# A DiT block pair on one core: attention in one written order with two-bank PSUM tiles, modulation units beside the block pairs, and the last norm in two halves

## The chip, the core and the metric

The kernel runs on one core of one Trainium2 chip. The metric is the device time of one execution in microseconds (us). The kernel before took 1587.46 us, the median of three runs (1584.85 to 1589.65). A profile is one more execution, recorded by the hardware profiler; its span runs from the first to the last instruction, and the execution's own time lies a little above it.

## What is computed

Two layers on 256 latent tokens and 256 context tokens of width 1024. Layer 0 is swiglu, short convolution, swiglu; layer 1 is swiglu, grouped-query attention (8 query heads of 128, 2 key/value heads, 512 keys), swiglu. Layer 1 after the attention works on the latent tokens alone. Cut to what matters here:

```python
mod  = (silu(c) @ mod_w[i] + mod_b[i])          # shift, scale, gate for each of three sublayers
modc = (silu(c_ctx) @ mod_w[i] + mod_b[i])      # the same for the context stream
...
lat = lat + 0.5 * gate * swiglu(rms(lat) * g * (1 + scale) + shift, w13, w2)
...
q = rope(rms(h @ w_q)); k = [rms(hc @ w_k), rope(rms(h @ w_k))]; v = [hc @ w_v, h @ w_v]
p = softmax(q k^T / sqrt(128))
lat = lat + gate * ((p v) @ w_o)
...
lat = lat + 0.5 * gate * swiglu(rms(lat) * g * (1 + scale) + shift, w13, w2)
```

Everything is float32. A product is made on TensorE from operands that are each split in a high part (rounded to fp32r by a copy on ScalarE) and a low part (the rest, a subtraction on VectorE); three matmuls (high*high, high*low, low*high) add up to one product.

## The kernel before

Activations are kept transposed, as eight tiles of 128 features by tokens. Each weight tile of 1 MB comes by DMA from the SP queue (load_raw, L92, three buffers), is split (split, L97) by ScalarE at L98 and VectorE at L99 into halves "wh" and "wl" of 1024 columns (four buffers of each), and is used by mm3 (L118), three matmuls at L122 to L124. An engine runs its instructions in one order, which a scheduler made ahead of time out of the program's text by its own estimate of times; an instruction that waits holds all behind it on its engine. Where the text says tc.manual_schedule, the named engines keep the order of the text.

**Modulation.** The 224 modulation units are VectorE dot products of 128x1024 (mod_unit, L136, instruction at L142, tile "junk"), whose weights go through the same raw buffers. next_unit (L169) issues one; tick(n) (L179) adds n to what is owed and issues units while one is owed; mod_ready (L186) issues whatever a value still lacks. Ticks stand in the projections (1.5 or 1.9 an output tile), in the convolution (6 a tile), four in the attention's projections, 2 a head in the attention, 1 an output tile in the attention's output projection, and 1 a block in the last swiglu.

**Block pairs.** In the three swiglus on 512 tokens most of the hidden blocks are worked with seven products of half size instead of eight (class Pair, L539): head, five, six, seven and four each issue products and the small VectorE and ScalarE steps between them. In the loop of ffn (L611) the pair before is finished (seven, four) amid the products of the next.

**Attention.** PSUM is divided into six one-bank tiles (psm) and two (pss). For each head, scores (L1033) makes two 128x512 score tiles "psc" (one per query tile), for each the row maximum (L1042), the scaled negative of it (L1044), the exponential with its row sum on ScalarE (L1050), a reciprocal (L1054) and the division on POOL (L1058). turn (L1062) transposes the probabilities by eight matmuls into "pt" and splits them (L98, L99); mix (L1078) multiplies with the values into "pav" and splits the result into "a". Projections of the values (v_proj, L966) for the context tokens stand between the first heads. The text runs two heads of scores ahead; the scheduler picked the order. Then wo, the output projection: eight output tiles "py" of 24 matmuls each, each added to x (gated, L1119), after which x, scaled but not yet normed, is split into "xa".

**The last swiglu.** 22 blocks. The first four (first_mm, L1170) work on "xa", so that they can begin before the norm is known, and are corrected afterwards by the reciprocal of the norm "rl" (first_post, L1194). In block 1 the norm is made (rms_inv), and after it the normed operand "h": for each of eight tiles a product on VectorE (L256), a shift on ScalarE (L1226) and a low part on VectorE (L1227). From block 4 on, mm2 (L1106) does with "h" and one 512-column matmul (L1107) and one of 256 (L1108) what takes three elsewhere.

Of the kernel before, what the change touches and what calls it, by code (L numbers as in the profile page):

```python
# [9 lines left out]
F32 = mybir.dt.float32  # L10
# [6 lines left out]
P = 128  # L17
D = 1024
KT = D // P
S = 256  # L20
# [7 lines left out]
EPS = 1e-6  # L28
WARM = 36
# [12 lines left out]
def hybrid_kernel(ctx: ExitStack, tc: tile.TileContext, a: dict, out: bass.AP):  # L42
# [7 lines left out]
    psm = ctx.enter_context(tc.tile_pool(name="psm", bufs=6, space=bass.MemoryType.PSUM))  # L50
    pss = ctx.enter_context(tc.tile_pool(name="pss", bufs=2, space=bass.MemoryType.PSUM))
# [8 lines left out]
    def psum(s="ps"):  # L60
        return psm.tile([P, T2], F32, tag="mm", name=nm(s))

    def psmall(s="pq"):
        return pss.tile([P, T2], F32, tag="sm", name=nm(s))
# [114 lines left out]
    def tick(n):  # L179

        owed[0] += n
        while (jobs or units) and owed[0] >= 1:
            owed[0] -= 1
            next_unit()
# [348 lines left out]
    class Pair:  # L533
# [66 lines left out]
        def seven(self):  # L600
            self.prod(self.p, "S3", "T3", False)
            nc.vector.tensor_tensor(
                out=self.u[:, S:], in0=self.p, in1=self.gm[:, S:], op=ALU.add
            )
# [300 lines left out]
    pqs = pss.tile([P, T2], F32, tag="sm", name="pqs")  # L905
# [60 lines left out]
    def v_proj(tt):  # L966
        if tt % 2 == 0:
            vt.append(new_pair("v"))
        ps = psum("pv")
# [62 lines left out]

    def scores(hd):  # L1033
        kv = hd // (HEADS // KVH)
        r_ = []
        for qt in range(2):
            o = (hd % 2) * S + qt * P
            ps = psum("psc")
            mm3(ps, tuple(t[:, o : o + P] for t in qs[hd // 2]), ks[kv], True, True)
            ci = hd * 2 + qt  # L1040
            mx = ap.tile([P, 1], F32, name=nm("mx"), tag="mx", bufs=4)
            nc.vector.reduce_max(mx, ps, axis=AX.X)  # L1042
            nb = ap.tile([P, 1], F32, name=nm("nb"), tag="nb", bufs=4)
            nc.vector.tensor_scalar(  # L1044
                out=nb, in0=mx, scalar1=scq[:, ci : ci + 1], scalar2=-1.0,
                op0=ALU.mult, op1=ALU.mult,
            )
            e = tp.tile([P, T2], F32, name=nm("e"), tag="sg", bufs=3)
            sm = ap.tile([P, 1], F32, name=nm("sm"), tag="smx", bufs=4)
            nc.scalar.activation(  # L1050
                out=e, in_=ps, func=AF.Exp, scale=scq[:, ci : ci + 1], bias=nb, accum_out=sm
            )
            r = ap.tile([P, 1], F32, name=nm("r"), tag="r", bufs=4)
            nc.vector.reciprocal(r, sm)  # L1054
            if qt == 0:
                pn2 = hot("pn", F32)
            pn = pn2[:, qt * T2 : qt * T2 + T2]
            nc.gpsimd.tensor_scalar(out=pn, in0=e, scalar1=r, scalar2=None, op0=ALU.mult)  # L1058
            r_.append(pn)
        return r_  # L1060

    def turn(pn):  # L1062
        pth, ptl = (hot(t).rearrange("p (b q) -> p b q", q=S) for t in ("pth", "ptl"))
        for qt in range(2):
            pt = psum("pt")
            for kt in range(4):
                nc.tensor.transpose(
                    pt[:, kt * P : kt * P + P], pn[qt][:, kt * P : kt * P + P], ident
                )
            split(  # L1070
                pth[:, :, qt * P : qt * P + P], ptl[:, :, qt * P : qt * P + P],
                pt.rearrange("p (k q) -> p k q", k=4),
            )
        return pth, ptl

    aos, at = [], []

    def mix(hd, pt):  # L1078
# [4 lines left out]
        po = psum("pav")  # L1083
        for kt in range(4):
            vw = tuple(t[:, kv * P : kv * P + P] for t in vs[kt])
            mm3(po[:, :S], vw, (pt[0][:, kt, :], pt[1][:, kt, :]), kt == 0, kt == 3)
        o = (hd % 2) * S
        ah, al = (t[:, o : o + S] for t in at[-1])
        split(ah, al, po[:, :S])
        aos.append((ah, al))  # L1090

    pns, pts = {0: scores(0)}, {}
    v_proj(2)
    v_proj(3)
    pns[1] = scores(1)
    for hd in range(HEADS):
        if hd + 2 < HEADS:
            pns[hd + 2] = scores(hd + 2)
        pts[hd] = turn(pns.pop(hd))
        if hd:  # L1100
            mix(hd - 1, pts.pop(hd - 1))
        tick(2)
    mix(HEADS - 1, pts.pop(HEADS - 1))


# [32 lines left out]
    wo = by_pairs("wo")  # L1138
    for m in range(KT):
        if m == KT - 2:  # L1140
            ready()
        w = wo(m)
        ps = psum("py")
        for k in range(KT):
            mm3(ps[:, :S], w(k), aos[k], k == 0, k == KT - 1)
        gated(m, ps[:, :S], gate)
        square_add(m, 0, S)
# [10 lines left out]
        tick(1)  # L1158
# [46 lines left out]
    ht = []  # L1205
    for i in range(NM):
# [3 lines left out]
        if i < 4:  # L1210
# [6 lines left out]
            if i == 1:  # L1217
                for q in range(4):
                    t = hot("h")
                    ht.append(t)  # L1220
                    for k in (2 * q, 2 * q + 1):
                        o = (k % 2) * T2
                        hi, lo = t[:, o : o + S], t[:, o + S : o + T2]
                        u = scaled(0, k, A, ris)
                        b = B[:, k, :1]
                        nc.scalar.activation(out=hi, in_=u, func=AF.Identity, bias=b)  # L1226
                        nc.vector.scalar_tensor_tensor(  # L1227
                            out=lo, in0=u, scalar=b, in1=hi.bitcast(F32),
                            op0=ALU.add, op1=ALU.subtract,
                        )  # L1230
# [120 lines left out]
```

## Time and profile before

| | |
|---|---|
| runs | 1584.85, 1587.46, 1589.65 us |
| the profiled execution's own time | 1589.78 us |
| its span | 1588.0 us |
| mean granted TensorE clock | 0.995 |
| VectorE busy | 1319.8 us (83%) |
| ScalarE busy | 738.2 us (46%) |
| POOL busy | 29.8 us (2%) |

A line of the timeline reads: start, duration, engine, operation and source line, the tile written and those read, shapes, and how many instructions were merged; in square brackets stands how long the engine had been idle before, and what ended that. Times of a merged line run from the first start to the last end. Matmul durations include a pipeline's latency, so that consecutive matmuls overlap; how far apart they start is what counts.

### The profile page before, as it was taken

To read this page: it belongs to the slowest core of one execution; us is meant where nothing else is said; L and a number is where in the kernel's file an instruction comes from. 1 tells how busy PE (TensorE), PEld (TensorE's weight loads), DVE (VectorE), ACT (ScalarE), POOL (GpSimd) and SP (SyncE) were. 2 spreads that over 40 slices of the span, in tenths; PEclk is the share of its full clock that TensorE was granted. 3 is DMA by queue.
4 is the path that set the end of the run, shared out by engine and by line. 5 is a ranking of instruction groups with operands and counts; after the bars stand their busy time and mean duration, and the time that the engine had idled before them with its cause. 6 is when DMAs were issued, how large, how long until landed. Compare 5 with 4: busy or idle time off the path is not lost.

```text
span 1588.0 us, 25040 instructions
## 1 busy us (share of the span) xinstructions
PE 1565.0 (99%) x10210; PEld 1423.9 (90%) x10210; DVE 1319.8 (83%) x2029; ACT 738.2 (46%) x1180; POOL 29.8 (2%) x20
## 2 busy tenths in 40 slices
PE   8999999999999999999999999999999999899998
PEld 6788998998888899989899899899899898888887
DVE  5778778879998879799798899898898899976654
ACT  5532452544322356335345375335255455655543
POOL 0000000000000000000000000000000005200000
PEclk9999999999999999999999999999999999999999
DMA  8545234234565412452342423443433654645552
GB/s 319 181 174 201 92 115 167 104 117 162 186 214 193 177 65 95 142 200 104 130 177 102 160 103 107 158 161 107 175 133 122 235 186 149 234 156 186 186 202 90
DMA packets 38419, 248.74 MB, mean 157 GB/s; under 512 B 5280, under 2 KB 7072, under 8 KB 11936
## 3 DMA queue, kind: packets, MB, share of 16 engines
q1 hardware_dynamic: 35712, 245.38, 43.5%
q10 hardware_dynamic: 2592, 1.76, 0.4%
q8 instruction: 80, 1.31, 0.3%
q14 instruction: 35, 0.29, 0.1%
HBM read 244.77 MB, written 1.05 MB: 155 GB/s over the span
## 4 chain that ended last, share of the span: by engine, by line
PE 93%; DVE 3%; ACT 2%; DMA 1%; issue 1%; POOL 0%; DVEq 0%; POOLq 0%; ACTq 0%
PE py L122 9%; PE py L123 9%; PE py L124 9%; PE p L124 7%; PE p L123 7%; PE p L122 7%; PE q L122 5%; PE q L123 5%; PE q L124 5%; PE py L1107 3%; PE pg L1107 2%; PE pu L1107 2%; PE pg L122 2%; PE pg L123 1%; PE pg L124 1%; PE pu L124 1%
## 5 line engine op out<-in xcount | busy, mean ns | idle before, releaser
L98 ACT ACTIVATE wh<-wr 128x1024 fp32r<-128x1024 f32 (+2 forms) x276 | 277.2, 1015 | 352.2 <-PE py L123 81.2
L99 DVE TENSOR_TENSOR wl<-wr,wh 128x1024 fp32r<-128x1024 f32 (+2 forms) x276 | 319.7, 1166 | 78.4 <-ACT wh L98 71.0
L142 DVE CUSTOM_DVE_ANT_0 junk<-wr,scbc,modb 128x1024 bf16<-128x1024 f32 x224 | 286.8, 1280 | 25.0 <-DMA wr<-in_modT 22.2
L123 PE MATMUL py<-gl,wh 128*128 128x512 f32 (+1 forms) x570 | 213.3, 374 | 0.0
L122 PE MATMUL py<-gh,wh 128*128 128x512 f32 (+1 forms) x570 | 213.3, 374 | 0.0
L124 PE MATMUL py<-gh,wl 128*128 128x512 f32 (+1 forms) x570 | 213.0, 374 | 0.0
L99 DVE TENSOR_TENSOR wl<-ws,wh 128x1024 fp32r<-128x1024 f32 x108 | 131.3, 1223 | 28.6 <-ACT wh L98 28.1
L98 ACT ACTIVATE wh<-ws 128x1024 fp32r<-128x1024 f32 x108 | 113.4, 1058 | 75.1 <-DVE ws L563 32.5
L124 PEld LDWEIGHTS py<-gh,wl 128*128 128x128 f32 x570 | 107.3, 188 | 19.1
L122 PEld LDWEIGHTS py<-gh,wh 128*128 128x128 f32 x570 | 107.4, 188 | 18.5
L123 PEld LDWEIGHTS py<-gl,wh 128*128 128x128 f32 x570 | 107.4, 188 | 18.2
L123 PE MATMUL p<-tl,wh 128*128 128x256 f32 x432 | 122.2, 283 | 0.0
L124 PE MATMUL p<-th,wl 128*128 128x256 f32 x432 | 122.2, 283 | 0.0
L122 PE MATMUL p<-th,wh 128*128 128x256 f32 x432 | 122.2, 283 | 0.0
L122 PE MATMUL q<-bh,wh 128*128 128x256 f32 x320 | 90.6, 283 | 0.0
L123 PE MATMUL q<-bl,wh 128*128 128x256 f32 x320 | 90.6, 283 | 0.0
L124 PE MATMUL q<-bh,wl 128*128 128x256 f32 x320 | 90.6, 283 | 0.0
L122 PEld LDWEIGHTS p<-th,wh 128*128 128x128 f32 x432 | 82.9, 192 | 0.3
L123 PEld LDWEIGHTS p<-tl,wh 128*128 128x128 f32 x432 | 82.9, 192 | 0.3
L124 PEld LDWEIGHTS p<-th,wl 128*128 128x128 f32 x432 | 82.9, 192 | 0.0
L446 DVE SCALAR_TENSOR_TENSOR x<-py,G,x 128x256 f32<-128x256 f32 x144 | 62.9, 477 | 6.3 <-PE py L124 6.0
L557 DVE TENSOR_TENSOR ws<-wr 128x1024 f32<-128x1024 f32 x54 | 65.7, 1218 | 0.0
(296 smaller groups left out, 4181.1 us busy)
## 6 DMA issues: line engine op xcount, KB each, us to landing
wr<-in_w SPq DMA_DIRECT2D x88, 1024.0 KB, 4.9
wr<-in_modT SPq DMA_DIRECT2D x64, 1024.0 KB, 4.8
wr<-in_w2b SPq DMA_DIRECT2D x24, 896.0 KB, 4.6
wr<-in_w2a SPq DMA_DIRECT2D x12, 1024.0 KB, 4.8
wr<-in_mod SPq DMA_DIRECT2D x8, 1024.0 KB, 6.1
wr<-in_cw_cx SPq DMA_DIRECT2D x8, 1024.0 KB, 4.8
wr<-in_w2l SPq DMA_DIRECT2D x8, 1024.0 KB, 4.8
wr<-in_cw_b SPq DMA_DIRECT2D x4, 1024.0 KB, 4.9
```

Source lines behind the costliest of these rows:

```text
L98: nc.scalar.activation(out=hi, in_=src, func=AF.Copy)
L99: nc.vector.tensor_tensor(out=lo, in0=src, in1=hi.bitcast(F32), op=ALU.subtract)
L122: nc.tensor.matmul(ps, wh, mh, start=first, stop=False, **kw)
L123: nc.tensor.matmul(ps, wh, ml, start=False, stop=False, **kw)
L124: nc.tensor.matmul(ps, wl, mh, start=False, stop=last, **kw)
L142: nc.vector.tensor_tensor_reduce(out=junk, in0=raw[:, j * D : j * D + D], in1=scbc[:, v, :], scale=1.0, scalar=modb[:, l, col : col + 1], ...
L446: nc.vector.scalar_tensor_tensor(out=x[:, m, s * S : s * S + S], in0=ps[:, o : o + S], scalar=g[:, m, s : s + 1], in1=x[:, m, s * S : s * ...
L557: tt(out=sm.rearrange("p (a b c) -> p a b c", a=2, b=2)[:, :, 0, :], in0=a21.unsqueeze(1).to_broadcast([P, 2, T2]), in1=self.raw[:, T2 : 3 ...
L1107: nc.tensor.matmul(ps, w[0], m, start=first, stop=False, skip_group_check=True)
```

## The change

- A pool of PSUM can be closed and another opened in its place (use_banks); the option reuse_waits="tile" makes a new tile wait for the old tiles that it overlaps. During the attention PSUM is two score tiles of two banks each, one transposition tile of two banks, and two one-bank tiles for the products with the values. After the second output tile of wo the old division comes back.
- scores makes both query tiles into one two-bank tile, with one row maximum of 128x2x512, one negation and one reciprocal for both. The division on POOL is in place. turn, rest, out_hi and out_lo are the parts of the two splits.
- TensorE, VectorE and ScalarE follow the text's order through the whole attention, the first two tiles of wo included. wo's first weights are loaded and split ahead of it; a one-column exponential ahead of it loads the table.
- The ticks of the attention and of wo go; a tick of 0.5 comes behind the addition in seven in the block pairs' loop, queued right behind that addition.
- In the last swiglu five blocks work on "xa" instead of four. The normed operand is made in two halves, after blocks 1 and 2 and behind their corrections: for a half, one product on VectorE of 128x1024, for each tile two shifts on ScalarE (one rounded, one not), and for each two tiles one subtraction on VectorE.

```diff
+FIRST = 5
+ORDERED = {mybir.EngineType.PE, mybir.EngineType.DVE, mybir.EngineType.Activation}
...
+    def use_banks(*pools):
+        stage.close()
+        for name, bufs in pools:
+            banks[name] = stage.enter_context(
+                tc.tile_pool(
+                    name=name, bufs=bufs, space=bass.MemoryType.PSUM, reuse_waits="tile"
+                )
+            )
+
+    use_banks(("psm", 6), ("pss", 2))
...
-    def tick(n):
+    def tick(n, behind=None):
...
+            if behind is None:
+                next_unit()
+            else:
+                with tc.issue_after(behind.ins):
+                    next_unit()
...
-                        prev.seven()
+                        tick(0.5, prev.seven())
...
+    warm = ap.tile([P, 1], F32, name="warm", tag="warm", bufs=1)
+    nc.scalar.activation(out=warm, in_=scq[:, :1], func=AF.Exp, scale=0.0)
+    use_banks(("psc", 2), ("ptp", 1), ("pav", 2))
...
+    wo = by_pairs("wo")
+    w01 = [wo(m) for m in range(2)]
...
     def scores(hd):
...
+        ps = double("psc", "psc")
         for qt in range(2):
...
+            mm3(ps[:, qt, :], tuple(t[:, o : o + P] for t in qs[hd // 2]), ks[kv], True, True)
+        nc.vector.reduce_max(mx, ps, axis=AX.X)
...
+    with tc.manual_schedule(engines=ORDERED):
+        scores(0)
+        scores(1)
+        exps(0)
+        exps(1)
+        v_proj(2)
+        scores(2)
+        turn(0, 0)
+        rest(0, 0)
+        exps(2)
+        v_proj(3)
+        turn(0, 1)
+        rest(0, 1)
+        for hd in range(1, HEADS):
+            turn(hd, 0)
+            if hd + 2 < HEADS:
+                scores(hd + 2)
+            turn(hd, 1)
+            rest(hd, 0)
+            if hd > 1:
+                out_hi(hd - 2)
+                out_lo(hd - 2)
+            rest(hd, 1)
+            if hd + 2 < HEADS:
+                exps(hd + 2)
+            mix(hd - 1)
+        py2 = double("psc", "py")
...
+        out_hi(HEADS - 2)
+        out_lo(HEADS - 2)
+        wo_mm(0, range(6))
+        mix(HEADS - 1)
+        out_hi(HEADS - 1)
+        out_lo(HEADS - 1)
+        wo_mm(1, range(6))
+        for m in range(2):
+            wo_mm(m, range(6, KT))
...
-        tick(2)
...
         gated(m, ps[:, :S], gate)
+        if m == 1:
+            use_banks(("psm", 6), ("pss", 2))
...
-        tick(1)
...
+    def norm_half(hf):
+        u = hot("u", F32)
+        ks = slice(4 * hf, 4 * hf + 4)
+        nc.vector.tensor_tensor(
+            out=u.rearrange("p (k t) -> p k t", k=4), in0=x[:, ks, :S],
+            in1=ris.unsqueeze(1).to_broadcast([P, 4, S]), op=ALU.mult,
+        )
+        for q in range(2):
...
+            for j in range(2):
...
+                nc.scalar.activation(
+                    out=t[:, j * T2 : j * T2 + S], in_=u[:, c], func=AF.Identity, **kw
+                )
+                nc.scalar.activation(out=u[:, c], in_=u[:, c], func=AF.Identity, **kw)
...
-        if i < 4:
+        if i < FIRST:
...
             if i:
                 for one in held:
                     first_post(*one, ris)
                 held = []
+            if i in (1, 2):
+                norm_half(i - 1)
```

In the new functions turn(hd, qt) issues the four transpositions of one query tile and the ScalarE copy that is its high part, rest(hd, qt) the VectorE subtraction that is its low part, exps(hd) two exponentials, one reciprocal and the two divisions on POOL, out_hi and out_lo the two parts of the split of a head's result.

More of the change, by code (lines that the diff above doesn't have):

```diff
@@ L968, in v_proj @@
             vt.append(new_pair("v"))
-        ps = psum("pv")
+        ps = psum("pv") if tt < 2 else banks["pav"].tile([P, T2], F32, tag="t", name=nm("pv"))
         for k in range(KT):
@@ L1036, in scores @@
         for qt in range(2):
             o = (hd % 2) * S + qt * P
[L1038 to L1046, printed above, removed]
-            )
@@ L1058, in scores @@
[L1058 to L1072, printed above, removed]
-            )
-        return pth, ptl
@@ new lines, in exps @@
+    def exps(hd):
+        ps, nb = es[hd]
+        sc = scq[:, 2 * hd : 2 * hd + 2]
+        e = es[hd] = hot("e", F32)
+        sm = ap.tile([P, 2], F32, name=nm("sm"), tag="smx", bufs=3)
+        for qt in range(2):
+            nc.scalar.activation(
+                out=e[:, qt * T2 : qt * T2 + T2], in_=ps[:, qt, :], func=AF.Exp,
+                scale=sc[:, qt : qt + 1], bias=nb[:, qt : qt + 1],
+                accum_out=sm[:, qt : qt + 1],
+            )
+        r = ap.tile([P, 2], F32, name=nm("r"), tag="r", bufs=3)
+        nc.vector.reciprocal(r, sm)
+        for qt in range(2):
+            c = slice(qt * T2, qt * T2 + T2)
+            nc.gpsimd.tensor_scalar(
+                out=e[:, c], in0=e[:, c], scalar1=r[:, qt : qt + 1], scalar2=None, op0=ALU.mult
+            )
@@ new lines, in turn, with rest @@
+    def turn(hd, qt):
+        e = es[hd]
+        if qt == 0:
+            pts[hd] = hot("pth"), hot("ptl"), double("ptp", "pt")
+        hi, pt = pts[hd][0], pts[hd][2]
+        for kt in range(4):
+            nc.tensor.transpose(
+                pt[:, qt, kt * P : kt * P + P],
+                e[:, qt * T2 + kt * P : qt * T2 + kt * P + P], ident,
+            )
+        nc.scalar.activation(
+            out=hi[:, qt * T2 : qt * T2 + T2], in_=pt[:, qt, :], func=AF.Copy
+        )
+    def rest(hd, qt):
+        hi, lo, pt = pts[hd]
+        c = slice(qt * T2, qt * T2 + T2)
+        nc.vector.tensor_tensor(
+            out=lo[:, c], in0=pt[:, qt, :], in1=hi[:, c].bitcast(F32), op=ALU.subtract
+        )
@@ L1082, in mix @@
             at.append((t[:, :T2], t[:, T2:]))
-        po = psum("pav")
+        po = pos[hd] = banks["pav"].tile([P, T2], F32, tag="t", name=nm("po"))
+        by_k = [t.rearrange("p (q k t) -> p k q t", q=2, k=4) for t in pts[hd][:2]]
+        p3 = po[:, :S].rearrange("p (q t) -> p q t", q=2)
         for kt in range(4):
             vw = tuple(t[:, kv * P : kv * P + P] for t in vs[kt])
-            mm3(po[:, :S], vw, (pt[0][:, kt, :], pt[1][:, kt, :]), kt == 0, kt == 3)
+            mm3(p3, vw, tuple(t[:, kt] for t in by_k), kt == 0, kt == 3)
@@ L1087, in mix @@
         o = (hd % 2) * S
[L1088 to L1101, printed above, removed]
-        tick(2)
-    mix(HEADS - 1, pts.pop(HEADS - 1))
+        aos.append(tuple(t[:, o : o + S] for t in at[-1]))
@@ L1141, in hybrid_kernel @@
             ready()
[L1142 to L1145, printed above, removed]
+        if m < 2:
+            ps = py2[:, m, :]
+        else:
+            w = wo(m)
+            ps = psum("py")
+            for k in range(KT):
+                mm3(ps[:, :S], w(k), aos[k], k == 0, k == KT - 1)
         gated(m, ps[:, :S], gate)
+        if m == 1:
+            use_banks(("psm", 6), ("pss", 2))
         square_add(m, 0, S)
```

75 lines of the change are left out of this document (41 added, 34 removed).

## The prediction

> **What bounds the kernel now.** The first thing read was the page's busy times.
>
> ```profile
> span 1588.0 us, 25040 instructions
> PE 1565.0 (99%) x10210; PEld 1423.9 (90%) x10210; DVE 1319.8 (83%) x2029; ACT 738.2 (46%) x1180; POOL 29.8 (2%) x20
> ```
>
> TensorE (PE) is busy in 1565.0 of 1588.0 us. The change removes no product, so it can win only where PE stands idle (at most 23 us, some of it at start and end) or runs at a lower clock. Second came the list of PE's waits; three of its rows:
>
> ```profile
> PE pg L1107 <- ACT wh L98: 3.2, 1, 3.2
> PE pt L1067 <- POOL pn L1058: 3.0, 3, 2.0
> ...
> PE py L124 <- DVE wl L99: 1.4, 1, 1.4
> ```
>
> The largest lie in the two stages that the change rewrites: the attention (transpositions waiting for POOL, wo waiting for its weights' low half) and the last swiglu. The third view was the timeline of PE in the attention.
>
> ```profile
> 1319.72 0.40 PE L123 MATMUL psc<-kl,qh 128*128 128x512 f32 x1
> ...
> 1334.74 0.83 PE L1067 MATMUL pt<-ident,pn 128*128 128x128 f32 x4 [1.96 <-POOL pn L1058]
> ...
> 1336.87 0.41 PE L124 MATMUL pav<-pth,vl 128*128 128x256 f32 x1
> 1337.08 0.41 PE L122 MATMUL pav<-pth,vh 128*128 128x256 f32 x1
> ...
> 1345.04 0.63 PE L1067 MATMUL pt<-ident,pn 128*128 128x128 f32 x4 [1.04 <-DVE ptl L99]
> 1345.55 0.39 PE L122 MATMUL pav<-pth,vh 128*128 128x256 f32 x1
> 1345.78 0.28 PE L123 MATMUL pav<-ptl,vh 128*128 128x256 f32 x1
> ...
> 1346.97 0.28 PE L124 MATMUL pav<-pth,vl 128*128 128x256 f32 x1
> 1347.09 0.40 PE L122 MATMUL psc<-kh,qh 128*128 128x512 f32 x1
> ...
> 1348.25 0.40 PE L124 MATMUL psc<-kh,ql 128*128 128x512 f32 x1
> ...
> 1367.53 0.39 PE L124 MATMUL py<-a,wl 128*128 128x256 f32 x1 [1.43 <-DVE wl L99]
> ```
>
> What the reader is to see: 256-column matmuls start 0.119 us apart (1345.78 to 1346.97, ten steps), 512-column ones 0.232 (1347.09 to 1348.25, five steps), four transpositions take 0.51. After the idle 1.96 us the matmuls start 0.21 apart: the clock has fallen too. After idle stretches of 1.04 and 1.43 it has not. The other engines' rows for the same stage:
>
> ```profile
> 1344.22 1.28 DVE L99 TENSOR_TENSOR ptl<-pt,pth 128x512 fp32r<-128x512 f32 x2
> 1344.82 0.68 DVE L99 TENSOR_TENSOR ptl<-pt,pth 128x512 fp32r<-128x512 f32 x1
> 1345.41 0.41 DVE L99 TENSOR_TENSOR a<-pav,a 128x256 fp32r<-128x256 f32 x1
> ...
> 1350.12 1.28 DVE L1042 TENSOR_REDUCE mx<-psc 128x1 f32<-128x512 f32 x2
> 1351.32 0.33 DVE L1044 TENSOR_SCALAR nb<-mx,scq 128x1 f32<-128x1 f32 x2
> 1351.57 1.27 DVE L142 CUSTOM_DVE_ANT_0 junk<-wr,scbc,modb 128x1024 bf16<-128x1024 f32 x1
> ...
> 1329.75 0.77 ACT L1050 ACTIVATE e<-psc,nb,scq 128x512 f32<-128x512 f32 x1
> 1332.87 1.07 ACT L98 ACTIVATE pth<-pt 128x512 fp32r<-128x512 f32 x2
> L1058 POOL TENSOR_SCALAR pn<-e,r x16: 1561/1566/2642, 1325.9 to 1360.3; 128x512 f32<-128x512 f32 x16
> ```
>
> VectorE (DVE) spends 1.2 us on a modulation unit between steps that PE waits for; the text puts sixteen there.
>
> **The attention, rewritten.** A head costs PE 8 transpositions (1.02), 6 score matmuls (1.39) and 12 of 0.119 (1.43), together 3.8 us; POOL 2 x 1.57 = 3.1; ScalarE two exponentials (1.6), two copies (1.07) and one smaller copy, about 3.0. DVE has, in the order written, the maximum of 1024 columns (two of 512 take 1.20 to the next start; I take 1.16), one negation (0.12, half of 1351.32 to 1351.57), a subtraction (0.60, the step 1344.22 to 1344.82), the smaller one for the head two back (0.34, an estimate from its 0.41 less the 0.07 by which such steps overlap) and a last subtraction (0.68). None of these sums is the period, because a loop runs through two engines: the transposition tile has one buffer, so the next head's first transposition waits for the last subtraction of this head, and that stands on DVE behind the maximum, which waits for the scores, which PE issues behind the first transpositions. Around it: 0.14 from the subtraction's end to PE (1344.22 + 0.68 = 1344.90 to 1345.04), 0.51, scores to their end 1.56 (1347.09 to 1348.25 + 0.40), 1.16, 0.12, 0.60, 0.34, 0.68: **5.1 us a head**, with PE idle for 1.3 of them. It holds for the five heads 1 to 5. For head 6 there are no scores: 0.14 + 1.02 + 0.54 (copy, half of 1.07) + 0.34 + 0.34 + 0.68 = 3.1, I take 3.2.
>
> Before the loop: at 1319.72 four matmuls of the first scores are left (0.93), then the second scores (1.39), a value projection of 24 matmuls (2.86), scores (1.39), transpositions (0.51), projection (2.86), transpositions (0.51), copy, subtraction and the way back (0.54 + 0.68 + 0.14): 1331.5. Five periods and 3.2: 1360.2. From there PE runs through to the second wo tile: 0.14 + 1.02 + 12 + 18 + 12 + 18 + 12 matmuls (72 x 0.119 = 8.57) = 9.7: 1369.9. The third wo tile takes PSUM that the first two held, so it waits for the second's addition to x, a DVE step of the 128x256 kind: 0.41 + 0.14 and the last matmul's tail (0.28 - 0.12), 0.7 us of new wait: 1370.6. In the trace of before, the last swiglu's first matmul gives the same point (its row stands below): 1390.5 less six tiles of 24 matmuls (17.1) = 1373.4. **The attention gains 2.8 us**, and its expected larger gain is eaten by the loop of 5.1.
>
> Unknown is on which old tile the first score tile's banks fall; if on the last value projection's, its eviction comes first, 0.54 + 0.68 + 0.14 = 1.4 at most, and nothing if not. I take nothing, since the old tiles are eight and one is late. wo's earlier weights cost nothing that I can place: ScalarE and DVE do those splits anyway. The exponential's table is loaded once in both.
>
> **Modulation.** By a count through the text, 24 ticks go and 46 half ticks (6 + 6, 5 + 6 + 6, 5 + 6 + 6 calls) come, 23 units; by the end of the attention's projections 216 units are issued where 206 were. The 216 are all that wo needs; the last eight fall into mm2 blocks. What they meet there and in the pairs:
>
> ```profile
> L142 DVE CUSTOM_DVE_ANT_0 junk<-wr,scbc,modb 128x1024 bf16<-128x1024 f32 x224 | 286.8, 1280 | 25.0 <-DMA wr<-in_modT 22.2
> ...
> 720.00:760.00 40.00, 40.00 (x336) 40.00 (x335) 36.67 (x47) 23.25 (x37) 0.00 (x0) 1.00 0.29 100
> 720.00:760.00 40.00, 0.00 (x0) 1.00 0.29 100
> ...
> 1445.00:1500.00 55.00, 55.00 (x314) 47.70 (x313) 36.32 (x59) 32.50 (x59) 0.00 (x0) 1.00 0.54 182
> ```
>
> The second and third rows are one stretch of pairs, all engines and then the units alone: PE 40.00, DVE 36.67, no unit. A pair is 84 matmuls, 10.0 us; half a unit each is 4 x 0.5 x 1.2 = 2.4 more, 39.1 of 40. That still fits, and part of the 36.67 is work ahead for the projection, so I take 0; the bound is a whole unit each, 28 us, and gets a rival. In the mm2 stretch DVE is busy 36.32 of 55, so eight units and their four loads of 1 MB (transfer engines half busy, 0.54) lie beside PE.
>
> **The last swiglu.** The rows of PE, DVE and ScalarE there:
>
> ```profile
> L122 PE MATMUL pg<-xa,wh x32: 276/282/419, 1390.5 to 1419.5; 128*128 128x258 f32 x32
> ...
> 1412.90 0.50 PE L1107 MATMUL pg<-h,wh 128*128 128x512 f32 x1 [3.18 <-ACT wh L98]
> 1413.59 0.40 PE L122 MATMUL pu<-xa,wh 128*128 128x258 f32 x1
> ...
> 1417.01 0.30 PE L124 MATMUL pg<-xa,wl 128*128 128x258 f32 x1
> ...
> 1420.47 0.40 PE L1107 MATMUL pg<-h,wh 128*128 128x512 f32 x1
> 1420.82 0.40 PE L1107 MATMUL pu<-h,wh 128*128 128x512 f32 x1
> ...
> 1401.73 1.28 DVE L256 SCALAR_TENSOR_TENSOR t<-x,A,rl 128x256 f32<-128x256 f32 x3 [1.21 <-ACT rl L1214]
> 1411.88 1.22 DVE L99 TENSOR_TENSOR wl<-wr,wh 128x1024 fp32r<-128x1024 f32 x1
> ...
> 1405.52 1.30 ACT L1226 ACTIVATE h<-t,mod 128x256 fp32r<-128x256 f32 x3
> 1406.84 1.28 ACT L1200 ACT_TABLE_LOAD   x1
> 1411.81 1.04 ACT L98 ACTIVATE wh<-wr 128x1024 fp32r<-128x1024 f32 x1
> ```
>
> PE stands 3.18 us in block 3, whose low weights ("wl") start on DVE only at 1411.88, behind ten microseconds of norm and corrections; then sixteen matmuls take 1413.59 to 1417.01, 3.42 where 1.90 is usual: 1.5 more. Together 4.7. After the change DVE has before block 3's weights two corrections (four steps of some 0.35 each, 2.8) and one half of the norm (1.16 + 2 x 0.60 = 2.4): from 1401.73 to 1406.9; the weights end at 1409.2. PE wants them after three blocks of 48 matmuls and 0.45 for the norm's own, 1390.5 + 17.6 = 1408.1. So about **1.1 us of wait stay**, too little for the clock to fall. ScalarE sets the other bound: table 1.28, eight shifts 3.4, two corrections 1.4, two weight halves 2.0 from 1401.7 end at 1409.8, DVE's last half at 1411.0: 2.9 of wait and perhaps the clock again. The fifth early block costs 48 x 0.119 = 5.71 against sixteen steps of 0.35 (1420.47 to 1420.82) = 5.60: 0.1. The gain is 4.7 - 1.1 - 0.1 = **3.5**, between 0.2 and 4.6.
>
> **The sum**: 1588.0 - 2.8 - 3.5 = 1581.7 for the span; 1.78 lie around the span in the profiled execution (1589.78), which was 2.3 above the median, so against the median 1587.46 - 6.3 = **1581.2 us**.
>
> **Rivals.** *Shorter loop.* If the transposition tile comes free bank by bank, its first bank waits only for the first subtraction: 0.34 + 0.68 drop out, 4.1 a head, five times 1.0: 1576.2. For it: every instruction that touches the tile keeps to one bank. Against: a tile is one thing to its pool.
>
> *The wait at the end stays.* The norm now takes twice the ScalarE shifts (16 instead of 8, 3.4 us more), on the engine that the 3.18 us row names: 3.3 of the 3.5 lost, 1584.5.
>
> *The clock.* PE is idle 1.3 us in every period. Only the 1.96 us gap was followed by a low clock here, 1.43 was not; but these repeat. At 0.21 instead of 0.119 a step the 0.51 and 1.39 on the loop grow by some 1.5, five times: 1588.7. The Trainium skill, TensorE: Matmul & The Clock Gate, bears on both sides: its Part 1 says that a wholly idle window of about 3.4 us lowers the clock, which the 1.96 us gap here contradicts; its paragraph on a second failure mode says that short idle spells between groups of matmuls can make the clock swing.
>
> *Slower: units beside the pairs hold PE.* A unit queued right behind the addition delays by 1.2 us the weight splits behind it; PE, at 40.00 of 40, has no slack to make it good. If half of each of 23 units shows, 13.8 us: 1595.0. It decides from 0.48 us a unit (11 us, the gain and the bound below). For: DVE at 36.67 without any. Against: the weights have four buffers, and runs of units now pass the projections without a PE wait.
>
> **Chances.** What a measurement of this kernel can tell from no change is about 0.3%, 4.8 us: below 1582.7 is faster. The forecast 0.40 (1578 to 1585: 0.28 faster, 0.12 same), shorter loop 0.25 (faster), wait stays 0.10 (same), clock 0.10 (same), units 0.15 (slower). Faster 0.53, same 0.32, slower 0.15. The range reaches from the short loop with all of the last wait gone (1576.2 - 1.1, and 2 for the other waits of the attention) to the clock with a third of the last rival's price: 1573 to 1593.
>
> **What would show it.** Right: PE's wait for the transposition tile names the second subtraction, transpositions of one head start 5.1 apart, the wo tile after the second waits some 0.7, the 3.18 us row is near 1.1 and no slow matmuls follow it. Pairs show no PE wait and no DVE share of 40 in 40. Wrong: periods of 4.1, matmuls 0.21 apart inside the attention, or PE waits on "wl" in the pairs.

## The result, and the profile after

The changed kernel takes 1599.7 us, the median of four runs (1597.0 to 1603.71), against 1586.82 for the kernel before in four (1584.85 to 1589.65): a ratio of 1.0079, 95% interval 1.0061 to 1.0098. It is slower by about 13 us, where 6 us faster was forecast, and it lies above the range. The profiled execution took 1598.72 us, 8.9 more than the profiled one of before. The page's first rows of the changed kernel, and the list of TensorE's waits (for what, in all, how often, the longest):

```profile
span 1596.9 us, 25044 instructions
PE 1564.9 (98%) x10226; PEld 1426.5 (89%) x10226; DVE 1314.2 (82%) x1995; ACT 742.1 (46%) x1189; POOL 26.0 (2%) x20
```

```profile
PE pt L1102 <- DVE ptl L1113: 9.4, 7, 2.4
PE pg L136 <- ACT wh L112: 7.0, 2, 6.3
...
PE psc L136 <- ACT e L1083: 1.6, 1, 1.6
PE pt L1102 <- ACT pth L1106: 1.6, 2, 0.8
```

PE is busy as long as before (1564.9 against 1565.0 us), so all of the loss is new idle time. It lies in the two rewritten stages. The waits in the attention add up to some 13.6 us (these, and 1.0 for x before the third wo tile), where the kernel before had 7.8: the 3.0 and 1.4 shown ahead of the result, two smaller ones of 0.5 and 0.4, and these:

```profile
PE pt L1067 <- DVE ptl L99: 1.4, 2, 1.0
PE pav L122 <- ACT pth L98: 1.1, 1, 1.1
```

In the last swiglu one wait of 6.3 us stands where 3.2 stood. The two differences, 5.8 and 3.1, make up the 8.9 us by which the span grew. The timeline of PE in the attention of the changed kernel:

```profile
1318.91 0.40 PE L136 MATMUL psc<-kh,qh 128*128 128x512 f32 x1
...
1326.27 0.50 PE L136 MATMUL psc<-kh,qh 128*128 128x512 f32 x1 [1.58 <-ACT e L1083]
...
1334.47 1.08 PE L1102 MATMUL pt<-ident,e 128*128 128x128 f32 x4 [2.37 <-DVE ptl L1113]
...
1336.20 0.63 PE L138 MATMUL psc<-kh,ql 128*128 128x512 f32 x1
1336.63 0.63 PE L136 MATMUL psc<-kh,qh 128*128 128x512 f32 x1
...
1340.72 0.63 PE L1102 MATMUL pt<-ident,e 128*128 128x128 f32 x4 [0.95 <-DVE ptl L1113]
...
1345.87 0.63 PE L1102 MATMUL pt<-ident,e 128*128 128x128 f32 x4 [1.26 <-DVE ptl L1113]
...
1361.32 0.63 PE L1102 MATMUL pt<-ident,e 128*128 128x128 f32 x4 [1.27 <-DVE ptl L1113]
1362.72 0.63 PE L1102 MATMUL pt<-ident,e 128*128 128x128 f32 x4 [0.78 <-ACT pth L1106]
...
1365.79 0.63 PE L1102 MATMUL pt<-ident,e 128*128 128x128 f32 x4 [1.00 <-DVE ptl L1113]
...
1377.41 0.39 PE L136 MATMUL py<-a,wh 128*128 128x256 f32 x1 [0.97 <-DVE x L1196]
```

Four things are to be seen. The loop over the heads begins at 1334.47, not at 1331.5. Its period is 5.15 us (1340.72 to 1345.87, and so on to 1361.32), as worked out; only the first one is longer, 6.25, because the matmuls behind the gap of 2.37 run slowly (512-column ones 0.43 apart). Head 6, which has no scores, takes 4.47 (1361.32 to 1365.79): its second four transpositions wait 0.78 for ScalarE's copy "pth" of the first four, which went into the other bank, and those of head 7 do the same. And the third wo tile starts at 1377.41, against 1373.4 before: the attention has lost 4.0 us in this trace where 2.8 were to be won.

The last swiglu, on PE and then on ScalarE:

```profile
1419.83 0.58 PE L136 MATMUL pg<-xa,wh 128*128 128x258 f32 x1 [6.29 <-ACT wh L112]
...
1424.14 0.42 PE L136 MATMUL pg<-xa,wh 128*128 128x258 f32 x1
1424.35 0.42 PE L137 MATMUL pg<-xa,wh 128*128 128x258 f32 x1
...
1405.99 1.28 ACT L1279 ACT_TABLE_LOAD   x1
...
1411.97 1.08 ACT L1300 ACTIVATE h<-u,mod,A 128x256 fp32r<-128x256 f32 x2
...
1417.30 1.04 ACT L112 ACTIVATE wh<-wr 128x1024 fp32r<-128x1024 f32 x1
1418.24 0.59 ACT L1303 ACTIVATE u<-u,mod,A 128x256 f32<-128x256 f32 x1
1418.73 2.94 ACT L112 ACTIVATE wh<-wr 128x1024 fp32r<-128x1024 f32 x3
```

ScalarE works without a break from 1405.99 on, and one half of block 3's weights comes at 1417.30, the one that PE waits for at 1418.73: behind all sixteen shifts of the norm (one takes 0.59, a pair of them 1.08, so that they start 0.50 apart) and three corrections. PE stands 6.29 us for them, and the matmuls behind it start 0.21 apart, at a granted clock of 0.50 (1419.80 to 1424.50). The pairs, in turn, show nothing; one stretch of them, all engines and then the modulation units alone:

```profile
720.00:760.00 40.00, 40.00 (x336) 40.00 (x335) 35.93 (x47) 22.92 (x37) 0.00 (x0) 1.00 0.37 125
720.00:760.00 40.00, 2.57 (x4) 1.00 0.37 125
```

With two units in it PE is busy in all 40 us, as it was without any.

### The profile page after: what moved, and what is told of

Same layout as the page of the kernel before. It is cut to its first block, busy times and chain, and to the rows that moved or that the text cites. A ratio compares the mean times of both kernels' runs of the same rounds, so it can differ in the third digit from the quotient of the medians.

```text
span 1596.9 us, 25044 instructions
## 1 busy us (share of the span) xinstructions
PE 1564.9 (98%) x10226; PEld 1426.5 (89%) x10226; DVE 1314.2 (82%) x1995; ACT 742.1 (46%) x1189; POOL 26.0 (2%) x20
## 4 chain that ended last, share of the span: by engine, by line
PE 91%; DVE 4%; ACT 3%; DMA 1%; issue 1%; POOL 0%; DVEq 0%; ACTq 0%
PE py L136 8%; PE py L137 8%; PE py L138 8%; PE p L138 6%; PE p L137 6%; PE p L136 6%; PE q L138 5%; PE q L136 5%; PE q L137 5%; PE py L1183 3%; PE pu L1183 2%; PE pg L1183 2%; PE pg L136 2%; PE pg L137 2%; PE pg L138 2%; PE pu L137 2%
```

## Which part of the change costs what: three runs

Three kernels separate the parts. The first is the changed one with the old norm; the second the kernel before with the new norm alone; the third the kernel before with the ticks moved alone.

```diff
 changed kernel, old norm
-FIRST = 5
+FIRST = 4
-            if i in (1, 2):
-                norm_half(i - 1)
+            if i == 1:
+                for q in range(4):
...
```

> The changed kernel with the last swiglu's norm and its four early blocks as they were before; attention and modulation stay changed. Theory A (the 8.9 us that the span grew lie 4.3 in the attention and 4.6 in the last swiglu, where sixteen ScalarE shifts of 0.50 stand ahead of block 3's weight copies): the span falls from 1596.9 to about 1592.3, the 6.29 us wait in the last swiglu goes back to some 3.2, and the attention still ends 4.3 late. Rival B (the last swiglu waits because it inherits late weights from the rewritten attention): the wait stays near 6 and the span near 1597.

> The kernel before with the last swiglu's new norm and five early blocks alone. Theory A: wait of some 6.3 us before block 3 at a low clock after it, span about 1592.6, 4.6 above before. Rival B: no change beyond 1 us, or the 3.5 us gain that was predicted.

> The kernel before with the ticks moved alone: the attention and wo as before but without their 24 ticks, half ticks in the pairs. Theory A (units beside pairs cost nothing; before the attention both traces are level): no later start of the attention, and the old attention, rid of 16 units of 1.2 us on DVE, is some 3 to 6 us shorter, span 1582 to 1585. Rival C (units beside the pairs hold PE): span above 1588, with PE waits on low weight halves in the pairs.

| kernel | median, us | ratio to before | 95% interval |
|---|---|---|---|
| before, same chip | 1588.24 | 1 | |
| changed, old norm | 1594.68 | 1.0045 | 1.0028 to 1.0063 |
| before, new norm alone | 1594.32 | 1.0034 | 1.0022 to 1.0046 |
| before, ticks moved alone | 1585.33 | 0.9981 | 0.9966 to 0.9996 |

With the old norm the wait at block 3 is 3.2 us again. With the new norm alone, in the old attention, it is the same 6.29; the timeline of PE in that kernel:

```profile
1415.35 0.58 PE L122 MATMUL pg<-xa,wh 128*128 128x258 f32 x1 [6.29 <-ACT wh L98]
```

So the norm's loss is its own and needs nothing of the attention. Moving the ticks alone gains 2.9 us: the pairs carry the units for nothing, and the old attention, without them on VectorE, lets PE wait less: 4.1 us in all instead of 7.8, of which 1.9 instead of 3.0 are for POOL. By the medians, the ticks give -2.9, the new norm +6.1, and the rewritten attention (the first row less the third of the variants) +9.4; together 12.6, and the changed kernel's own loss was 12.9. The parts add up, and the rewritten attention, taken by itself, is the largest of them.

## The attention: one tile, or the order?

The 0.78 waits on "pth" suggested that the two-bank tile is followed as one thing: a reader of one bank holds the writer of the other, and the other way round. In this run it became two one-bank tiles with the same space, in the kernel with the old norm.

```diff
-    use_banks(("psc", 2), ("ptp", 1), ("pav", 2))
+    use_banks(("psc", 2), ("ptp", 2), ("pav", 2))
...
-            pts[hd] = hot("pth"), hot("ptl"), double("ptp", "pt")
-        hi, pt = pts[hd][0], pts[hd][2]
+            pts[hd] = [hot("pth"), hot("ptl")]
+        pt = banks["ptp"].tile([P, T2], F32, tag="t", name=nm("pt"))
+        pts[hd].append(pt)
+        hi = pts[hd][0]
```

> As e1_old_norm, but the transposition tile of two banks is two tiles of one bank each. Theory D (the attention's period is the loop through the release of the two-bank tile): the period falls from 5.15 to about 4.1, and heads 6 and 7, where the second four transpositions wait for ScalarE's copy of the first bank, shrink from 4.4 to about 3.2 each; together 7 us less than e1, span about 1585. Rival E (the period is DVE's and ScalarE's work itself): period stays at 5.1, span as e1 within 1 us.

Measured: 1587.52 us, ratio 0.9998 (0.9985 to 1.0011), 7.2 us less than with the two-bank tile. The timeline of its PE:

```profile
1347.00 0.63 PE L1104 MATMUL pt<-ident,e 128*128 128x128 f32 x4 [0.52 <-DVE ptl L1115]
...
1351.40 0.63 PE L1104 MATMUL pt<-ident,e 128*128 128x128 f32 x4 [0.52 <-DVE ptl L1115]
```

The period falls from 5.15 to 4.40, the waits of 2.37 and 0.78 go, and what is left is 0.52 a head. The prediction's rival had 4.1 for this case; the rest was looked for in VectorE's order, where the first subtraction stands behind the maximum. The next run puts it ahead.

```diff
+            rest(hd, 0)
+            if hd + 2 < HEADS:
+                peak(hd + 2)
```

(peak is the row maximum and its negation, taken out of scores.)

> As e4_one_bank_pt, but on DVE the first subtraction of a head stands ahead of the maximum of the head two on. In e4 the period is 4.40 and PE waits about 0.5 a head for that subtraction, which stands behind the maximum. If the order on DVE is what is left of the loop, the period falls to PE's own 3.8 and the span by about 3, to 1579. If POOL or ScalarE sets it, the period stays at 4.4.

Measured: 1588.2 us, 0.9996 (0.9984 to 1.0009), no different from the kernel without this edit, and the period stays 4.40. In the loop of its timeline only the name in the brackets has changed:

```profile
1345.68 0.66 PE L1108 MATMUL pt<-ident,e 128*128 128x128 f32 x4 [0.50 <-POOL e L1096]
...
1350.07 0.66 PE L1108 MATMUL pt<-ident,e 128*128 128x128 f32 x4 [0.48 <-POOL e L1096]
```

The maximum now comes later, and with it the exponentials and POOL's divisions; half a microsecond of one wait became half a microsecond of another. This was a miss for the idea that VectorE's order holds the loop. What does hold it at 4.40 was not isolated.

Before the loop the scores of head 2 wait 1.58 us. VectorE's and ScalarE's timelines of the changed kernel say why:

```profile
1320.48 1.23 DVE L113 TENSOR_TENSOR wl<-wr,wh 128x1024 fp32r<-128x1024 f32 x1 [0.44 <-ACT wh L112]
...
1322.22 1.22 DVE L1069 TENSOR_REDUCE mx<-psc 128x2 f32<-128x1024 f32 x1
...
1324.07 0.63 ACT L112 ACTIVATE qh<-kn 128x512 fp32r<-128x512 f32 x1 [2.11 <-DVE kn L947]
1324.61 0.76 ACT L1083 ACTIVATE e<-psc,nb,scq 128x512 f32<-128x512 f32 x1
```

Head 2's score tile is head 0's, given back by head 0's exponentials; these stand on ScalarE behind the last rotated query, and their maximum on VectorE behind the low half of a wo weight. In the next run, wo's first weights are loaded in the loop, behind head 3, on top of the one-bank tiles.

```diff
-    w01 = [wo(m) for m in range(2)]
+    w01 = []
...
             mix(hd - 1)
+            if hd == 3:
+                w01.extend(wo(m) for m in range(2))
```

> As e4_one_bank_pt, but wo's first weights are loaded and split behind head 3 in the written order instead of ahead of the attention. Theory F (the head of the attention is late because wo's splits, 1.06 us on ScalarE and 1.22 on DVE each, stand in its way): PE's waits of 1.58 us before the third scores and the one before head 1 shrink, some 2 us. Rival G (it is late because the last query rotation stands on ScalarE and DVE ahead of the first exponential): the 1.58 us wait stays, span within 1 us of e4's 1582.3, or above it by what the splits cost in the loop.

Measured: 1588.65 us, 1.0004 (0.9992 to 1.0016). The wait fell from 1.58 to 0.45, so the weights were most of its cause, but the loop got a new one:

```profile
1331.13 0.50 PE L136 MATMUL psc<-kh,qh 128*128 128x512 f32 x1 [0.45 <-ACT e L1083]
...
1357.11 0.63 PE L1104 MATMUL pt<-ident,e 128*128 128x128 f32 x4 [3.52 <-DVE ptl L1115]
```

PE's waits in the attention add up to 7.4 us in both kernels. The splits are the same work on the same two engines in both places; in the fixed order they only chose whom they delayed. No third place in the text was tried.

## The last swiglu: how much ScalarE does, or when

The new norm has sixteen shifts on ScalarE where the old one has eight; and in the text the weights of block 3 stand behind both halves. Two runs, on the kernel before with the new norm alone, change one of these each. The first keeps the halves and the five blocks and makes each half from the old steps (eight shifts in all, the sums on VectorE):

```diff
-                nc.scalar.activation(out=u[:, c], in_=u[:, c], func=AF.Identity, **kw)
+                u = scaled(0, k, A, ris)
+                nc.scalar.activation(out=hi, in_=u, func=AF.Identity, bias=b)
+                nc.vector.scalar_tensor_tensor(
+                    out=lo, in0=u, scalar=b, in1=hi.bitcast(F32),
+                    op0=ALU.add, op1=ALU.subtract,
+                )
```

> The kernel before with five early blocks and the norm in two halves behind blocks 1 and 2, but made of the old steps (eight shifts on ScalarE instead of sixteen, two VectorE steps a tile). Theory H (the 6.29 us wait is the amount on ScalarE: sixteen shifts of 0.50 and the rest from 1405.99 to 1417.3 ahead of block 3's copies): with 4.7 us less on ScalarE the wait falls under 3.2 and the span to between 1585 and 1588. Rival I (it is the place: two halves behind the corrections hold back block 3's weights whatever they are made of): the wait stays above 5, span near 1592.

The second keeps the sixteen shifts and writes the load of blocks 2 and 3 ahead of the corrections and the halves:

```diff
+            if i in (1, 2):
+                early[i + 1] = load_w(a["w13"][1, 1, i + 1])
             if i:
                 for one in held:
                     first_post(*one, ris)
```

> The kernel before with the last swiglu's change whole, but blocks 2 and 3 ask for the next block's weights ahead of their corrections and of the norm, so that the scheduler prefers their splits. Theory I (place): block 3's wait goes, some 4 us under e2_norm_only and about the kernel before or better, 1584 to 1588. Theory H (amount): ScalarE has as much to do, the wait moves to block 4 or 5 and the span stays within 2 of e2's 1592.4.

| kernel | median, us | ratio to before | 95% interval |
|---|---|---|---|
| new norm alone (above) | 1594.32 | 1.0034 | 1.0022 to 1.0046 |
| halves of old steps | 1586.52 | 0.9987 | 0.9977 to 0.9998 |
| weights ahead | 1585.37 | 0.9975 | 0.9963 to 0.9988 |

Either edit is enough to take most of the 6.29. In the first the wait is 1.74 and now for VectorE, which has the sums; in the second, with every shift still there, it is 1.58 and 0.57. The rows of PE, first of the one, then of the other:

```profile
1415.78 0.39 PE L124 MATMUL pg<-xa,wl 128*128 128x258 f32 x1 [1.74 <-DVE wl L99]
```

```profile
1408.57 0.39 PE L122 MATMUL pg<-xa,wh 128*128 128x258 f32 x1 [1.58 <-ACT wh L98]
...
1415.12 0.39 PE L122 MATMUL pg<-xa,wh 128*128 128x258 f32 x1 [0.57 <-ACT c L1181]
```

And ScalarE with the weights ahead:

```profile
1405.44 0.59 ACT L1222 ACTIVATE h<-u,mod,A 128x256 fp32r<-128x256 f32 x1
1405.93 1.04 ACT L98 ACTIVATE wh<-wr 128x1024 fp32r<-128x1024 f32 x1
1406.88 0.59 ACT L1225 ACTIVATE u<-u,mod,A 128x256 f32<-128x256 f32 x1
...
1407.46 1.06 ACT L98 ACTIVATE wh<-wr 128x1024 fp32r<-128x1024 f32 x1
```

A weight half now goes between two shifts, after 6.5 us of ScalarE's work (the table load begins at 1399.45) instead of 11.3 (1405.99 to 1417.30). The work is the same; the queue is in another order. From the stage's first matmul to the first of block 5 the traces have 39.48 us with the new norm alone, 32.03 with the halves of old steps and 32.73 with the weights ahead. Of the last one's 6.75 us some 4.1 are waits; the rest is mostly the low clock that stood behind the 6.29. The medians differ by 9.0, and where the other 2.2 lie is not shown (the last section has a candidate).

## Putting the parts together

Four more kernels test whether the findings add up: the moved ticks, the halves and the weights ahead in the old attention; the changed kernel with the two repairs (one-bank tiles, weights ahead); the first of these with halves of old steps; and with the old norm and four blocks, weights ahead.

```diff
 the changed kernel, mended: both edits shown above, and
+        w = early.pop(i) if i in early else load_w(a["w13"][1, 1, i])
```

> The kernel before with the modulation's units beside the block pairs, the halves of the norm with five early blocks, and the weights of the blocks behind the halves issued ahead of the corrections and of the halves; the attention is the old one. Theory I (place of the weights in ScalarE's queue): the two gains measured alone (0.9981 and 0.9975) stand at different places and add up: ratio 0.9956, 1579.8 us, with the waits of TensorE at blocks 3 and 4 together under 2.5 us. Rival K: the gain of the moved units is given back, because the units were what the old attention's engines had time for, and the ratio stays at 0.9975 or above.

> The changed kernel with two repairs: the transpositions' tile as two one-bank tiles, and the weights of the blocks behind the halves issued ahead of the corrections and of the halves. Theory D + I: the repair of the tile is worth 7 us (1594.7 to 1587.5 in the kernel with the old norm) and that of the weights 9 us (1594.3 to 1585.4 in the kernel with the norm alone); from 1599.7 that gives 1583.7 us, ratio 0.998, with the wait of 6.29 gone to 2 and the loop's period at 4.4. Rival L: something else of the changed kernel is still slow, and the ratio is 1.001 or more.

> As the kernel with the moved units, the halves and the weights ahead, but with the halves written with the old operations (eight shifts on ScalarE, the rest on VectorE). Theory M: with the weights ahead ScalarE's eight further shifts still hold 2 us (the waits of 1.58 and 0.57), and without them they go: 1577.5 us, ratio 0.994. Rival N: with the weights in their place the amount of ScalarE's work no longer counts, or VectorE's longer steps take its place (a wait for the wl of block 3, 1.74 us where the weights stood in the old place): 1579.8 to 1581.5, ratio 0.9955 or above.

> The kernel before with the modulation's units beside the block pairs, its old norm and four early blocks, and the weights of blocks 2 and 3 issued ahead of the norm and of the corrections. Theory P: the place of the weights in ScalarE's queue is all there is to gain at the last swiglu, and the norm in halves with five blocks adds nothing: the old norm's wait of 3.2 at block 3 goes, ratio 0.9955 as with the halves and the place (0.995). Rival Q: with four blocks the normed operand is needed one block sooner, and with the weights ahead of it ScalarE and VectorE bring it late, so that a wait for h or for a correction takes the place of the old one: ratio 0.9975 or above, and the halves have earned the rest.

| kernel | median, us | ratio to before | 95% interval |
|---|---|---|---|
| old attention, ticks moved, halves, weights ahead | 1579.78 | 0.995 | 0.9935 to 0.9966 |
| changed kernel, mended | 1582.99 | 0.9976 | 0.9965 to 0.9986 |
| the first, halves of old steps | 1582.91 | 0.9965 | 0.9954 to 0.9976 |
| the first, old norm | 1584.08 | 0.9972 | 0.9958 to 0.9985 |

The first is the fastest version measured: it beats both kernels, by 8 us the one before. The mended kernel came out where the two repairs put it (1583.7 was expected). So with the tile and the weights put right the change does pay; but its rewritten attention does not. The old attention without units has the same period as the written one, 4.4 us, in the first kernel's timeline. With units, in the trace of before, the same steps lie 5.1 apart. First the one, then the other:

```profile
1347.94 0.60 PE L1071 MATMUL pt<-ident,pn 128*128 128x128 f32 x4
...
1352.37 0.60 PE L1071 MATMUL pt<-ident,pn 128*128 128x128 f32 x4
```

```profile
1343.41 0.60 PE L1067 MATMUL pt<-ident,pn 128*128 128x128 f32 x4
...
1348.49 0.60 PE L1067 MATMUL pt<-ident,pn 128*128 128x128 f32 x4
```

The loop's whole gain came from taking the units out, which the scheduler's own order used as well. The lead of 3.2 us over the mended kernel agrees with the waits of PE in the two attentions: 1.9 for POOL, 1.1 for "ptl", 0.7 for "pth" and 0.4 for the exponentials, together 4.1, in the old order; 3.7 for "ptl", 1.6 for the exponentials, 1.1 for POOL and 1.0 for x, together 7.4, in the written one. Which of these an edit could take out was not tried.

The third kernel is unclear. Its trace has no wait at blocks 3 and 4, as the theory that ScalarE's amount still counts expected, but its median is 3.1 us above the first one's, above even what the rival had, and so speaks rather for the rival. In the fourth a wait for VectorE took the old one's place, with matmuls at a granted clock of 0.57 behind it (1408 to 1412). The rival had expected such a wait, if for h or a correction and not for a weight, and its 0.9975 is nearer to the 0.9972 measured than the theory's 0.9955: the halves seem to have earned the rest. The interval overlaps that of the first kernel (0.9958 to 0.9985 and 0.9935 to 0.9966), so this is not shown beyond the noise:

```profile
1408.04 0.58 PE L124 MATMUL pu<-xa,wl 128*128 128x258 f32 x1 [2.18 <-DVE wl L99]
```

## Why the prediction was wrong, point by point

- **The loop of 5.1 us: right.** Behind the first, the period is 5.15, the wait for "ptl" is 1.26 against the 1.3 given. The reason given for the tile, one buffer that the last subtraction gives back, holds, and the rival of a release bank by bank falls: only separate tiles did that, and then at 4.40 and not at 4.1, with a wait for VectorE in one order and for POOL in the other.
- **The start of the loop at 1331.5: wrong by 3.0.** The step summed PE's instructions and one copy and subtraction. It left out that head 2's scores take the tile of head 0 and wait for its exponentials (1.58), 0.21 behind POOL, and that the copy of the last transpositions stands on ScalarE behind head 2's exponentials (a wait of 2.37 where 0.54 + 0.68 + 0.14 = 1.36 were counted). The sentence "wo's earlier weights cost nothing that I can place" fails here: they could be placed.
- **Head 6: 3.2 taken, 4.47 measured.** The sum let both banks of a head run one behind the other on PE (1.02). The rule that the step itself used, that a tile is one thing, was not carried through: the second transpositions wait for the reader of the first. In the loop the scores hide it; in the last two heads nothing does, and head 7 has its 0.78 as well.
- **The wait at the third wo tile: right**, 0.97 against 0.7. The choice to take nothing for the score tiles' old banks was right too: no wait stands before the first scores.
- **The attention: the third wo tile at 1377.41 instead of 1370.6.** Of these 6.8 us, 3.0 are the start, 1.1 the first period at a low clock, 0.2 the other periods, 1.3 head 6, 0.8 head 7 and 0.3 the wait before that tile. By the medians the attention with its ticks taken out is 6.4 us slower than the one before (1594.68 against 1588.24) where 2.8 were to be won; against the old attention without ticks it is the 9.4 above. So what it was compared with was wrong too: the old loop was read with its units, and without them it is as short as any written here.
- **Modulation at nothing: right in the pairs** (PE 40.00 of 40) **and too low by 2.9 us of gain for the attention.** The rival that units beside the pairs hold PE, whose 1595.0 is the nearest number to the result, is wrong: alone, the move made the kernel faster.
- **The last swiglu: +6.1 instead of -3.5, and here the failed step is plain.** The prediction, in its count of what stands on VectorE and on ScalarE, put "two corrections and one half of the norm" ahead of block 3's weights. In the text the second half and the third corrections stand there as well, and the scheduler did not lift the weights over them. Its bound for ScalarE inherited this: eight shifts instead of sixteen (8 x 0.50 = 4.0 more), at 0.42 instead of 0.50 (0.6 for the first eight), two corrections instead of three (0.7). With these three put right its own sum ends at 1415.1, 7.0 behind the 1408.1 at which PE wants the weights; 6.29 was measured. The nearer bound of 1.1 was then taken from VectorE, whose low half the step blamed for the 3.18, while the row of before names ScalarE's high half. The rival "the wait stays" named the right cause, sixteen shifts, and lacked that PE waits for them all. For the size, the Trainium skill, ScalarE: Activation LUTs, in its section on what a table load costs, adds some 93 ns for each operand of an activation that is a pointer: the new shifts have two, scale and bias, where the old ones had the bias alone. The trace agrees: 0.50 apart against 1.30 for three, 0.40 or a little more each, before.
- **The clock: one of its signs came, at another price.** Behind the gap of 2.37 the matmuls ran at a granted clock of 0.50 (1335.00 to 1337.50), which cost the first period 1.1 us that no term has. The idle times of 1.26 in the other periods brought no slow matmuls, so the rival's five times 1.5 did not come. That a short wait is "too little for the clock to fall" is not safe all the same: with the old norm slow matmuls stood behind a gap of 0.78 (last section). Behind the 6.29 the slow steps came as they had behind the 3.18.

That the mended kernel lies at 1582.99 and the forecast was 1581.2 shows less than it seems: the terms differ, and errors cancel.

## What to carry to other kernels

Before a wait is priced, walk the text up to the load that ends it and count all that stands ahead of it on each engine: the same sixteen shifts cost 9 us less when two loads were written ahead of them. A tile of two PSUM banks was followed here as one thing, so that the reader of one bank held the writer of the other; that cost 0.75 us a head in the loop, and 0.78 in each of the two heads in which nothing else ran in between. Before a gain is given to a new order, the old order has to be tried with the same work taken out.

## What the runs showed of the hardware

The clock does not follow the length of the last gap alone. In the changed kernel the score matmuls behind the gap of 2.37 started 0.43 apart (its rows stand with the result). In the kernel with the old norm the same gap of 2.37 was followed by the usual 0.23, and slow matmuls came later, behind a gap of only 0.78. Its timeline of PE:

```profile
1336.28 0.63 PE L1102 MATMUL pt<-ident,e 128*128 128x128 f32 x4 [2.37 <-DVE ptl L1113]
...
1337.20 0.39 PE L138 MATMUL psc<-kh,ql 128*128 128x512 f32 x1
1337.43 0.40 PE L136 MATMUL psc<-kh,qh 128*128 128x512 f32 x1
...
1363.08 1.08 PE L1102 MATMUL pt<-ident,e 128*128 128x128 f32 x4 [0.78 <-ACT pth L1106]
...
1364.61 0.41 PE L136 MATMUL po<-pth,vh 128*128 128x256 f32 x1
1364.82 0.41 PE L137 MATMUL po<-ptl,vh 128*128 128x256 f32 x1
```

The slow stretch is some 3.2 us long here. The Trainium skill, TensorE: Matmul & The Clock Gate, Part 1, has the clock judged in windows that run freely, which would let one gap count at one time and not at another; but it asks for some 3.4 us of idleness, and no gap in either attention is that long.

And at a full granted clock (the 1.00 in these rows) the same stage ran in two speeds. The windows of 100 us in the last swiglu, first of the kernel with the subtraction first, then of the one with one-bank tiles, whose text is the same there:

```profile
1440.00:1540.00 100.00, 100.00 (x569) 86.71 (x568) 69.19 (x108) 57.56 (x99) 0.00 (x0) 1.00 0.57 207
```

```profile
1440.00:1540.00 100.00, 100.00 (x579) 88.32 (x578) 69.74 (x109) 57.86 (x100) 0.00 (x0) 1.00 0.60 213
```

569 against 579 matmuls is 1.7%. The two kernels enter the stage level (their last long wait ends at 1410.37 and 1410.34), so it accounts for the 2.9 us by which the two spans differ (1585.2 and 1582.3) while their medians are 0.7 apart. Of the fourteen kernels of this text eight were traced at 568 or 569, the one before and the changed one among them, and six at 578 or 579. What sets it, and whether it belongs to the execution or to the kernel, stays open with one trace of each. If it belonged to the kernel, it could make by itself the 2.9 us that the moved ticks gained (578 against 568), though PE's waits in the attention are 3.7 us shorter there too, and the 2.2 left open for the weights ahead (579 against 568). For this reason the verdicts above go by the runs' ratios and not by the spans, and the unclear third kernel of the last four, at 568, against 579 for the first, may owe its median to it.
